# The start of a hybrid attention/state-space block: first three projection units in written order, squares of x moved behind the splits, column table loaded first from another queue

## The chip, the cores and the metric

One core of a Trainium2 chip runs the whole kernel in one launch. The metric is the device time of one execution in microseconds (us), the median of several. Five engines work side by side, each through its own list of instructions in order: TensorE (PE, matrix products, with PEld for the loading of the stationary operand), VectorE (DVE), ScalarE (ACT), GpSimd (POOL) and SyncE (SP, which here only starts DMA transfers). They meet at semaphores.

## The reference

One layer, 512 positions, width 2048, all in float32:

```
u = rmsnorm(x, attn_norm_w)                 # x: 512 x 2048
z, xbc, dt, q, kc, vc, ks, vs, kw, vw, gate = split(u @ w_in)
y_ssd = ssd_mixer(z, conv4+silu(xbc), softplus(dt))    # chunked state-space scan, 16 heads
y_att = nsa_mixer(q, kc, vc, ks, vs, kw, vw, gate)     # compressed + selected + window attention
h = x + concat(y_ssd, y_att) @ w_out
v = rmsnorm(h, ffn_norm_w)
h = h + (silu(v @ w_gate) * (v @ w_up)) @ w_down       # hidden width 5632
return rmsnorm(h, final_norm_w)

rmsnorm(x, w) = x * rsqrt(mean(x*x over the width) + 1e-6) * w
```

The change touches only the first line and the first products `u @ w_in`.

## The kernel before, in words

**Numbers as two halves.** A float32 product is made of three products of a shorter type: each operand is split into a high part (ScalarE writes it, helper `a_hi`, L124) and a low part, the operand less its high part (VectorE, helper `lo`, L127). Then hi·hi, hi·lo and lo·hi are added up in PSUM (L234, L235, L236).

**The input projection.** x is held transposed, as 16 blocks `xt[:, k]` of 128 features by 512 positions. The norm's weight is a column table (`colc`, loaded from `cols`): `u_hi[k]` is the high part of x times its column (ScalarE, L124 `u<-xt,colc`), `u_lo[k]` the rest (VectorE, one scalar_tensor_tensor, L1818, which is L1843 in the changed kernel). The other factor of the norm, one number for each position, is applied after the product: `rms_stats` turns the sum of squares of x into the row `rrow` (flag "r1": four tiny products L282, then L283, a power on GpSimd L285, four transposes L289, a copy L290), and every result is multiplied by `rrow` as it leaves PSUM.

**Units.** The columns of `w_in` are taken in units of 128 (`run_unit`). A unit runs 16 steps k of three matmuls 128x128x512, 48 in all, into one PSUM bank: units 0 and 1 into the two banks `ps_t`, 2 and 3 into `ps_s`, from 4 on alternately into the two banks `ps_g`. The weights come in sub-blocks of 4 k (`wraw`, 256 KB, four buffers); `issue_split` splits one into `whi` and `wlo` (four buffers each) up to three sub-blocks ahead of the matmuls. From the seventh unit on, a unit first needs the unit two before it to have left its bank. Unit 0 holds dt and the gates, unit 1 is B, unit 2 C, units 3 to 6 the x columns of the state-space part's first group, and so on.

**Leaving PSUM.** A unit's `evac` is a generator that `Sched` advances by one step ("tick") after each k of the units that follow. All of them wait for "r1". For unit 0 it ends in a chain of small operations on `dtmp`; for units 1 to 12 it is a convolution of four taps (`conv`: `xpad<-ps,rrow`, then `cv`), a silu, splits and transposes. When these are there, the state-space core and the compression run as further generators between the matmuls.

**What sets the order.** The program is written down in one pass, and a scheduler of the framework then orders the instructions of each engine by its own simulation, except inside `manual_schedule`, where an engine keeps the written order. Before the change, the whole start is left to the scheduler, and PE's order is fixed from unit 25 on (`n_att`); the feed-forward part is fixed for all engines.

**The start before.** SP starts the transfers one after the other: the first weights, x block 0, the column table, x block 1, then pairs of x blocks with weights between. The squares of x are summed into `acc1` (ScalarE squares, GpSimd adds: even k) and `accb` (VectorE squares and adds: odd k), and the scheduler mixes these with the splits.

Of the kernel before, what the change touches and what calls it, by code (L numbers as in the profile page):

```python
# [8 lines left out]
F32 = mybir.dt.float32  # L9
F32R = mybir.dt.float32r  # L10
AF = mybir.ActivationFunctionType
ALU = mybir.AluOpType
AX = mybir.AxisListType

S, D, FF = 512, 2048, 5632
KD = D // 128
# [19 lines left out]
C_AN, C_FN, C_LN, C_SN, C_CW, C_CB, C_PE, C_W2 = 0, 16, 32, 48, 56, 104, 116, 148  # L36
# [29 lines left out]
U_Z = list(range(17, 25))  # L66
# [48 lines left out]
def body(ctx, tc, xT, w_in, w_out, w_gate, w_up, w_down, w1k, w1v, cols, rows, kst, out):  # L115
    nc = tc.nc
    act, dve, pool, pe = nc.scalar, nc.vector, nc.gpsimd, nc.tensor
    sch = Sched()

    def f(ap):  # L120
        return ap.bitcast(F32)

    def a_hi(dst, src, scale=1.0):
        act.activation(dst, src, AF.Copy, scale=scale)  # L124

    def lo(eng, dst, src, hi):
        eng.tensor_tensor(dst, src, f(hi), ALU.subtract)  # L127
# [4 lines left out]
    def mul(eng, o, a, b):  # L132
        eng.tensor_tensor(o, a, b, ALU.mult)  # L133

    def add(eng, o, a, b):
        eng.tensor_tensor(o, a, b, ALU.add)  # L136
# [8 lines left out]
    def ps_g():  # L145
        return ps("g", 2)

    def ps_s():
        return ps("s", 2)

    def ps_t():
        return ps("t", 2)
# [4 lines left out]
    def ps_m():  # L157
        return ps("m", 1)
# [11 lines left out]
    def open_pool(name, stack=None, **kw):  # L170
        es = ExitStack()
        pools[name] = (es, es.enter_context(tc.tile_pool(name=name, bufs=1, reuse_waits="tile", **kw)))
        return pools[name][1]

    def close_pool(name):
        pools.pop(name)[0].close()
# [18 lines left out]
    def issue_dma(upto):  # L195
        while st["dma"] <= min(upto, len(subs) - 1):
            i = st["dma"]
            src, n = subs[i]
            raw[i] = wp.tile([128, KSUB, 128], F32, tag="raw", name="wraw", bufs=4)
            nc.sync.dma_start(raw[i][:, :n, :], src)  # L200
            st["dma"] += 1

    def issue_split(upto):
        while st["split"] <= min(upto, len(subs) - 1):
            i = st["split"]
            issue_dma(i)
            n = subs[i][1]
            h = wp.tile([128, KSUB, 128], F32R, tag="whi", name="whi", bufs=4)
            l = wp.tile([128, KSUB, 128], F32R, tag="wlo", name="wlo", bufs=4)
            a_hi(h[:, :n, :], raw[i][:, :n, :])  # L210
            lo(dve, l[:, :n, :], raw[i][:, :n, :], h[:, :n, :])
            hi_t[i], lo_t[i] = h, l
            del raw[i]
            st["split"] += 1
            issue_dma(i + 3)

    def run_unit(u):
        if u.pre:
            u.pre()
        if u.need:  # L220
            sch.run_until(*u.need)
        n_u = st["unit"] = st.get("unit", 0) + 1
        if n_u > 6:
            sch.run_until(("evac", n_u - 2))
        p = ps_t() if n_u <= 2 else ps_s() if n_u <= 4 else ps_g()
        p = p[:, 0:u.cols[1] - u.cols[0]]
        for i, k0, n in u.sub:
            issue_split(i)
            for j in range(n):
                if j == 0:  # L230
                    issue_split(i + LEAD)
                k = k0 + j
                ah, al = [t[:, u.cols[0]:u.cols[1]] for t in u.rhs(k)]
                pe.matmul(p, hi_t[i][:, j, :], ah, start=(k == 0), stop=False)  # L234
                pe.matmul(p, hi_t[i][:, j, :], al, start=False, stop=False)  # L235
                pe.matmul(p, lo_t[i][:, j, :], ah, start=False, stop=(k == u.nk - 1))  # L236
                sch.tick()
            del hi_t[i], lo_t[i]

        def evac():  # L240
            yield from u.evac(p)
            sch.flags.add(("evac", n_u))
        sch.add(evac())


    colc = cst.tile([128, C_W2 + 4], F32, name="colc")
# [3 lines left out]
    rrow = cst.tile([128, 512], F32, name="rrow")  # L250
# [13 lines left out]
    def kcs(a, n):  # L264
        return kc[:, a - K_TRI:a - K_TRI + n]
# [6 lines left out]
    def col(c, n=1):  # L272
        return colc[:, c:c + n]
# [4 lines left out]
    def rms_stats(acc, n, dst, flag, gap=4):  # L278
        nb = acc.shape[1] // 128
        p = ps_m()  # L280
        for i in range(nb):
            pe.matmul(p[:, i:i + 1], acc[:, i * 128:(i + 1) * 128], ones[:, 0:1], start=True, stop=True)  # L282
        dve.tensor_scalar(rst[:, 0:nb], p[:, 0:nb], 1.0 / n, EPS, op0=ALU.mult, op1=ALU.add)  # L283
        r = rst[:, 4:4 + nb]
        pool.tensor_tensor(r, rst[:, 0:nb], nhalf[:, 0:nb], ALU.pow)  # L285
        yield gap
        p = ps_m()
        for i in range(nb):
            pe.transpose(p[:, i * 128:(i + 1) * 128], r[:, i:i + 1].to_broadcast([128, 128]), ident)  # L289
        act.activation(dst, p[:, 0:128 * nb], AF.Copy)  # L290
        sch.flags.add(flag)
# [9 lines left out]
    u_hi, u_lo = U[:, 0], U[:, 1]  # L301
# [244 lines left out]
    acc2 = cst.tile([128, 512], F32, name="acc2")  # L546
# [418 lines left out]
    def win(u):  # L965
        return w_in[u]
# [30 lines left out]
    order = [U_DTG]  # L997
# [6 lines left out]
    units = [Unit(win(u), KD, u_rhs, ev[u], pre=pre_att if u == U_VS[0] else (lambda: pre_ms()) if u == order[-1] else None) for u in order]  # L1004


    def pre_ms():
        P2["ms"] = [(U[:, 0, k], U[:, 1, k]) for k in range(8)]
        sch.run_until(("gp", 7))
        sch.add(ms_in())  # L1010
# [787 lines left out]

    xs = open_pool("xs")
    xt = xs.tile([128, KD, 512], F32, name="xt")  # L1800
    issue_dma(0)
    nc.sync.dma_start(xt[:, 0, :], xT[0])
    nc.sync.dma_start(colc[:, 0:C_PE], cols[:, 0:C_PE])
    nc.sync.dma_start(xt[:, 1, :], xT[1])
    for k in range(2, KD, 2):
        nc.sync.dma_start(xt[:, k:k + 2, :], xT[k:k + 2].rearrange("k p t -> p k t"))
        if k % 4 == 2:
# [1 line left out]
    nc.gpsimd.dma_start(rowc, rows.to_broadcast([128, 48]))  # L1809
    dve.memset(ones, 1.0)  # L1810
    act.activation(nhalf, ones[:, 0:4], AF.Copy, scale=-0.5)
    for k in range(KD):
        if k % 4 == 0:
            issue_split(k // 4)
        t = xt[:, k, :]
        w = col(C_AN + k)
        a_hi(u_hi[:, k, :], t, scale=w)
        dve.scalar_tensor_tensor(u_lo[:, k, :], t, w, f(u_hi[:, k, :]), op0=ALU.mult, op1=ALU.subtract)  # L1818
    acc1 = acc2
    accb = xs.tile([128, 512], F32, name="accb")  # L1820
    for k in range(KD):
        t = xt[:, k, :]
        if k < 2:
            act.activation((acc1, accb)[k], t, AF.Square)
        else:
            sq = xs.tile([128, 512], F32, tag=f"sq{k % 2}", name="sq", bufs=2)
            if k % 2:
                mul(dve, sq, t, t)
                add(dve, accb, accb, sq)
            else:  # L1830
                act.activation(sq, t, AF.Square)
                add(pool, acc1, acc1, sq)
    add(dve, acc1, acc1, accb)
    nc.sync.dma_start(ident, kst[:, 0:K_TRI])
    nc.sync.dma_start(tri, kst[:, K_TRI:K_AM])
    close_pool("xs")
    open_pool("kcp")
    open_pool("ssd")
# [1 line left out]
    sch.add(ssd_core())  # L1840
    sch.add(compress())
    sch.add(attention())
    first = units[0].evac  # L1843

    def ev_first(p):
        yield from rms_stats(acc1, D, rrow, "r1")
        yield from first(p)
    units[0].evac = ev_first
    n_att = order.index(U_Z[4])
    for n, u in enumerate(units[:n_att]):  # L1850
        if n == 4:
            nc.sync.dma_start(kcs(K_AM, NK - K_AM), kst[:, K_AM:NK])
            nc.sync.dma_start(colc[:, C_PE:C_W2], cols[:, C_PE:C_W2])
        run_unit(u)
    with tc.manual_schedule(engines={mybir.EngineType.PE}):
        sch.flags.add("order")
        for u in units[n_att:]:
# [90 lines left out]
```

## Time and profile before

| what | value |
|---|---|
| median of 3 runs | 2232.8 us (2230.76 to 2238.33) |
| the profiled execution | 2233.11 us, of which its span (first to last instruction) is 2231.3 us |
| PE busy | 2158.5 us, 97% of the span |
| DVE / ACT / POOL busy | 1793.7 / 1195.4 / 438.9 us |
| mean granted TensorE clock | 0.991 |
| moved by DMA | 427.14 MB, mean 191 GB/s |

Times are counted from the first instruction of the program. A row of the time line gives start, duration, engine, line, operation, and in brackets the idle time of that engine just before it and what ended it. A row of the table of stretches gives for each engine the busy time and the number of instructions, then the granted clock (PEclk), the mean busy share of the 16 DMA engines and the rate. Starts on PE are exact; ends are modelled, so two neighbouring starts say more than a duration.

### The profile page before, as it was taken

The page shows a single profiled execution, that of the slowest core. Times are in us where ns is not written, and L with a number is a line of the kernel's source. Part 1 is how long each engine was busy: PE and PEld are TensorE (multiplying, and loading weights), DVE is VectorE, ACT ScalarE, POOL GpSimd, SP SyncE. Part 2 cuts the span into 40 slices and gives each one's busy share as a digit, 9 for nine tenths or more (in the row PEclk, how much of TensorE's full clock was granted, in tenths as well). Part 3 has the DMA queues.
Part 4 walks back from the last instruction along what each step waited for, and adds up shares of the span by engine and source line. Part 5 has one row for each costly group of instructions (what it writes and reads, how often), then busy time and mean ns, then how long its engine had stood idle before and what let it go on. Part 6 is the DMA issues. An engine that isn't in the chain of part 4 may idle for free. (4 is left out here: it accounts for less than half of the span.)

```text
span 2231.3 us, 35003 instructions
## 1 busy us (share of the span) xinstructions
PE 2158.5 (97%) x12892; PEld 1897.8 (85%) x12892; DVE 1793.7 (80%) x2821; ACT 1195.4 (54%) x1991; POOL 438.9 (20%) x459
## 2 busy tenths in 40 slices
PE   7999999999999999999999999999999889999996
PEld 5888888888788887888888888888888889999996
DVE  7799766878886658888888888888887777888886
ACT  4564446676666657555555555555555333333453
POOL 2011224324431135000000000000000121211222
PEclk8999999999999999999999999999999999999998
DMA  5212342223464366778888787887878859686974
GB/s 178 92 68 80 116 156 84 75 93 109 140 207 118 105 211 210 228 217 253 230 236 236 218 246 222 254 229 223 243 218 264 319 189 309 201 275 185 297 187 135
DMA packets 174780, 427.14 MB, mean 191 GB/s; under 512 B 17248, under 2 KB 24432, under 8 KB 174608
## 3 DMA queue, kind: packets, MB, share of 16 engines
q1 hardware_dynamic: 101600, 251.97, 32.8%
q0 software_dynamic: 29712, 85.90, 18.8%
q10 hardware_dynamic: 43296, 87.04, 10.9%
q8 instruction: 101, 1.65, 0.3%
q14 instruction: 71, 0.58, 0.1%
HBM read 358.78 MB, written 62.39 MB: 189 GB/s over the span
## 5 line engine op out<-in xcount | busy, mean ns | idle before, releaser
L124 ACT ACTIVATE R<-Z 128x1024 fp32r<-128x1024 f32 (+4 forms) x458 | 415.9, 922 | 440.4 <-DVE Z L136 319.8
L127 DVE TENSOR_TENSOR R<-Z,R 128x1024 fp32r<-128x1024 f32 (+4 forms) x367 | 380.8, 1046 | 30.8 <-ACT R L124 19.6
L234 PE MATMUL ps_g<-u,whi 128*128 128x512 f32 x778 | 320.8, 412 | 0.0
L236 PE MATMUL ps_g<-u,wlo 128*128 128x512 f32 x778 | 306.2, 394 | 0.0
L235 PE MATMUL ps_g<-u,whi 128*128 128x512 f32 x778 | 304.9, 392 | 0.0
L1219 PE MATMUL ps_s<-u,R 128*128 128x512 f32 (+1 forms) x1160 | 252.9, 348 | 6.8 <-ACT A L1429 6.2
L1219 PEld LDWEIGHTS ps_s<-u,R 128*128 128x128 f32 x1160 | 187.7, 188 | 38.2 <-ACT A L1429 11.1
L127 DVE TENSOR_TENSOR wlo<-wraw,whi 128x512 fp32r<-128x512 f32 x211 | 162.0, 769 | 56.1 <-ACT whi L124 54.7
L124 ACT ACTIVATE whi<-wraw 128x512 fp32r<-128x512 f32 x211 | 131.4, 624 | 125.5 <-PE ps_g L235 82.2
L236 PEld LDWEIGHTS ps_g<-u,wlo 128*128 128x128 f32 x778 | 146.1, 188 | 31.8
L234 PEld LDWEIGHTS ps_g<-u,whi 128*128 128x128 f32 x778 | 146.7, 189 | 23.5
L235 PEld LDWEIGHTS ps_g<-u,whi 128*128 128x128 f32 x778 | 147.0, 189 | 21.1
L1219 PE MATMUL ps_t<-u,R 128*128 128x512 f32 (+1 forms) x600 | 131.4, 347 | 0.0
L1219 PE MATMUL ps_g<-u,R 128*128 128x512 f32 x584 | 131.3, 349 | 0.0
L1219 PE MATMUL ps_s<-T,R 128*128 128x512 f32 (+1 forms) x560 | 125.7, 349 | 1.0 <-DVE R L127 1.0
L1219 PE MATMUL ps_g<-T,R 128*128 128x512 f32 (+1 forms) x584 | 126.0, 346 | 0.7 <-DVE R L127 0.7
L1219 PE MATMUL ps_s<-V,R 128*128 128x512 f32 (+1 forms) x568 | 123.2, 347 | 0.0
L124 ACT ACTIVATE R<-A 128x1024 fp32r<-128x1024 f32 (+3 forms) x76 | 70.9, 933 | 85.9 <-DVE A L136 62.6
L127 DVE TENSOR_TENSOR E<-Z,R 128x1024 fp32r<-128x1024 f32 (+1 forms) x91 | 110.9, 1218 | 4.4 <-ACT R L124 4.1
L872 ACT ACTIVATE e<-e,em 128x128 f32<-128x128 f32 (+3 forms) x128 | 71.6, 559 | 76.1 <-DVE em L870 75.5
L136 DVE TENSOR_TENSOR A<-ps_g,A 128x512 f32<-128x512 f32 (+1 forms) x110 | 71.0, 652 | 50.7 <-PE ps_g L1219 38.6
L136 DVE TENSOR_TENSOR Z<-Z 128x1024 f32<-128x1024 f32 (+5 forms) x96 | 105.1, 1094 | 8.1 <-POOL E L136 5.2
(490 smaller groups left out, 5638.1 us busy)
## 6 DMA issues: line engine op xcount, KB each, us to landing
Z<-in_w_up SPq DMA_DIRECT2D x94, 512.0 KB, 5.0
Z<-in_w_gate SPq DMA_DIRECT2D x94, 512.0 KB, 6.5
wraw<-in_w_in SPq DMA_DIRECT2D x164, 256.0 KB, 2.6
g_d<-A ACTq DMA_DIRECT2D x22, 1792.0 KB, 15.1
Z<-in_w_up POOLq DMA_DIRECT2D x37, 512.0 KB, 7.7
Z<-in_w_gate POOLq DMA_DIRECT2D x37, 512.0 KB, 7.4
Z<-in_w_down SPq DMA_DIRECT2D x59, 320.0 KB, 6.2
Z<-in_w_down SPq DMA_DIRECT2D x41, 384.0 KB, 4.2
```

The lines of the kernel that those rows point to most:

```text
L124: act.activation(dst, src, AF.Copy, scale=scale)
L127: eng.tensor_tensor(dst, src, f(hi), ALU.subtract)
L136: eng.tensor_tensor(o, a, b, ALU.add)
L234: pe.matmul(p, hi_t[i][:, j, :], ah, start=(k == 0), stop=False)
L235: pe.matmul(p, hi_t[i][:, j, :], al, start=False, stop=False)
L236: pe.matmul(p, lo_t[i][:, j, :], ah, start=False, stop=(k == u.nk - 1))
L872: act.activation(e[:, 0:L], e[:, 0:L], AF.Exp, scale=-1.0, bias=m[:, 0:1], accum_out=m[:, 1:2])
L1219: pe.matmul(o, w, x, start=start, stop=(k == n - 1 and o is q), skip_group_check=not fresh[0])
```

## The change

1. The load of the column table is written first, and on ScalarE's queue instead of SP's; x blocks 0 and 1 then follow each other on SP.
2. The splits of x and of the first weights, and units 0, 1 and 2, are put inside `manual_schedule` for PE, ScalarE and VectorE: these three engines keep the written order there. First come all splits, with no square among them.
3. The squares of x become a generator, `x_squares`. It writes its first square 16 ticks after its start, which is the end of unit 0, and then one every second tick, beside units 1 and 2; all 16 squares are ScalarE's, all 15 additions VectorE's, into `acc2`. `accb` and GpSimd's seven additions are gone.
4. The statistics of the norm (`rms_stats`) wait for the flag "sq" that `x_squares` sets, instead of following unit 0 at once.

```diff
+    nc.scalar.dma_start(colc[:, 0:C_PE], cols[:, 0:C_PE])
     issue_dma(0)
-    nc.sync.dma_start(xt[:, 0, :], xT[0])
-    nc.sync.dma_start(colc[:, 0:C_PE], cols[:, 0:C_PE])
-    nc.sync.dma_start(xt[:, 1, :], xT[1])
+    for k in range(2):
+        nc.sync.dma_start(xt[:, k, :], xT[k])
...
-    for k in range(KD):
-        if k % 4 == 0:
-            issue_split(k // 4)
-        t = xt[:, k, :]
-        w = col(C_AN + k)
-        a_hi(u_hi[:, k, :], t, scale=w)
-        dve.scalar_tensor_tensor(u_lo[:, k, :], t, w, f(u_hi[:, k, :]), op0=ALU.mult, op1=ALU.subtract)
-    acc1 = acc2
-    accb = xs.tile([128, 512], F32, name="accb")
-    for k in range(KD):
-        t = xt[:, k, :]
-        if k < 2:
-            act.activation((acc1, accb)[k], t, AF.Square)
-        else:
-            sq = xs.tile([128, 512], F32, tag=f"sq{k % 2}", name="sq", bufs=2)
-            if k % 2:
-                mul(dve, sq, t, t)
-                add(dve, accb, accb, sq)
-            else:
-                act.activation(sq, t, AF.Square)
-                add(pool, acc1, acc1, sq)
-    add(dve, acc1, acc1, accb)
     nc.sync.dma_start(ident, kst[:, 0:K_TRI])
     nc.sync.dma_start(tri, kst[:, K_TRI:K_AM])
+
+    def x_squares():
+        yield 14
+        for k in range(KD):
+            yield 2
+            if k == 0:
+                act.activation(acc2, xt[:, k, :], AF.Square)
+            else:
+                sq = xs.tile([128, 512], F32, tag="sq", name="sq", bufs=2)
+                act.activation(sq, xt[:, k, :], AF.Square)
+                add(dve, acc2, acc2, sq)
+        sch.flags.add("sq")
...
+    def ev_first(p):
+        yield from sch.wait("sq")
+        yield 2
+        yield from rms_stats(acc2, D, rrow, "r1")
+        yield from first(p)
...
+    with tc.manual_schedule(engines={mybir.EngineType.PE, mybir.EngineType.Activation, mybir.EngineType.DVE}):
+        for k in range(KD):
+            if k % 4 == 0:
+                issue_split(k // 4)
+            t = xt[:, k, :]
+            w = col(C_AN + k)
+            a_hi(u_hi[:, k, :], t, scale=w)
+            dve.scalar_tensor_tensor(u_lo[:, k, :], t, w, f(u_hi[:, k, :]), op0=ALU.mult, op1=ALU.subtract)
+        sch.add(x_squares())
+        for u in units[:3]:
+            run_unit(u)
+        sch.run_until("sq")
     close_pool("xs")
...
     for n, u in enumerate(units[:n_att]):
...
-        run_unit(u)
+        if n >= 3:
+            run_unit(u)
```

**VectorE, from its first split on.** Names: `wlo` is the low half of a weight sub-block, `u` the low half of an x block, `sq`, `accb` and `acc` belong to the squares. Before:

```order
L127 TENSOR_TENSOR wlo<-wraw,whi 128x512
L1818 SCALAR_TENSOR_TENSOR u<-xt,colc,u 128x512 x2
L133 TENSOR_TENSOR sq<-xt 128x512
L136 TENSOR_TENSOR accb<-accb,sq 128x512
L1818 SCALAR_TENSOR_TENSOR u<-xt,colc,u 128x512 x2
L133 TENSOR_TENSOR sq<-xt 128x512
L127 TENSOR_TENSOR wlo<-wraw,whi 128x512
```

and now, where four such groups stand ahead of the first addition:

```order
L1843 SCALAR_TENSOR_TENSOR u<-xt,colc,u 128x512 x4
L127 TENSOR_TENSOR wlo<-wraw,whi 128x512
L1843 SCALAR_TENSOR_TENSOR u<-xt,colc,u 128x512 x4
L127 TENSOR_TENSOR wlo<-wraw,whi 128x512 x4
L136 TENSOR_TENSOR acc_96<-acc_96,sq 128x512 x2
L127 TENSOR_TENSOR wlo<-wraw,whi 128x512
```

The squares and additions that stood among the `u` rows have moved behind the last of them, two additions to each later weight split.

**ScalarE, from its first instruction on**, as a difference (- before, + now):

```order
+L1801 DMA colc<-in_cols 128x116
 L1811 ACT_TABLE_LOAD
 L1811 ACTIVATE colc<-ones 128x4
 L124 ACTIVATE whi<-wraw 128x512
-L1824 ACTIVATE acc_96<-xt 128x512
-L124 ACTIVATE u<-xt,colc 128x512 x2
-L1824 ACTIVATE accb<-xt 128x512
-L124 ACTIVATE u<-xt,colc 128x512 x2
-L1831 ACTIVATE sq<-xt 128x512
```

The load of the column table now stands at the head of ScalarE's list, and no square is left between the first `u` rows.

**PE, around the statistics of the norm (L282).** Before, in unit 1 (bank `ps_t`), after 90 large matmuls:

```order
L235 MATMUL ps_t<-u,whi 128x512
L236 MATMUL ps_t<-u,wlo 128x512
L282 MATMUL ps_m<-ones,acc_96 128x1 x4
L234 MATMUL ps_t<-u,whi 128x512
L235 MATMUL ps_t<-u,whi 128x512
```

and now in unit 3 (bank `ps_s`), after 160:

```order
L236 MATMUL ps_s<-u,wlo 128x512
L234 MATMUL ps_s<-u,whi 128x512
L282 MATMUL ps_m<-ones,acc_96 128x1 x4
L235 MATMUL ps_s<-u,whi 128x512
L236 MATMUL ps_s<-u,wlo 128x512
```

The statistics, and with them everything that waits for "r1", stand 70 large matmuls later in PE's list.

More of the change, by code (lines that the diff above doesn't have):

```diff
@@ L1811, in body @@
     act.activation(nhalf, ones[:, 0:4], AF.Copy, scale=-0.5)
-    for k in range(KD):
-        if k % 4 == 0:
-            issue_split(k // 4)
-        t = xt[:, k, :]
-        w = col(C_AN + k)
-        a_hi(u_hi[:, k, :], t, scale=w)
-        dve.scalar_tensor_tensor(u_lo[:, k, :], t, w, f(u_hi[:, k, :]), op0=ALU.mult, op1=ALU.subtract)
-    acc1 = acc2
-    accb = xs.tile([128, 512], F32, name="accb")
-    for k in range(KD):
-        t = xt[:, k, :]
-        if k < 2:
-            act.activation((acc1, accb)[k], t, AF.Square)
-        else:
-            sq = xs.tile([128, 512], F32, tag=f"sq{k % 2}", name="sq", bufs=2)
-            if k % 2:
-                mul(dve, sq, t, t)
-                add(dve, accb, accb, sq)
-            else:
-                act.activation(sq, t, AF.Square)
-                add(pool, acc1, acc1, sq)
-    add(dve, acc1, acc1, accb)
     nc.sync.dma_start(ident, kst[:, 0:K_TRI])
     nc.sync.dma_start(tri, kst[:, K_TRI:K_AM])
+    def x_squares():
[9 more added lines that the diff above has]
+        sch.flags.add("sq")
+    first = units[0].evac
+    def ev_first(p):
[3 more added lines that the diff above has]
+        yield from first(p)
+    units[0].evac = ev_first
+    n_att = order.index(U_Z[4])
+    with tc.manual_schedule(engines={mybir.EngineType.PE, mybir.EngineType.Activation, mybir.EngineType.DVE}):
[10 more added lines that the diff above has]
+        sch.run_until("sq")
     close_pool("xs")
@@ L1842, in body @@
     sch.add(attention())
[L1843 to L1849, printed above, removed]
     for n, u in enumerate(units[:n_att]):
```

## The prediction

> **What bounds the kernel now.** I read the page first, for the engine that is always busy, and then a table of stretches, for where it is not.
>
> ```profile
> PE 2158.5 (97%) x12892; PEld 1897.8 (85%) x12892; DVE 1793.7 (80%) x2821; ACT 1195.4 (54%) x1991; POOL 438.9 (20%) x459
> PEclk8999999999999999999999999999999999999998
> ```
> ```profile
> 0.00:32.00 32.00, 17.00 (x37) 11.15 (x38) 25.09 (x29) 20.27 (x34) 10.32 (x12) 0.74 0.66 226
> 32.00:100.00 68.00, 68.00 (x315) 56.23 (x313) 46.52 (x103) 29.55 (x46) 1.04 (x1) 0.99 0.29 100
> 100.00:200.00 100.00, 100.00 (x517) 83.86 (x516) 87.60 (x169) 52.28 (x82) 12.91 (x9) 1.00 0.22 77
> 200.00:331.00 131.00, 131.00 (x688) 111.15 (x685) 104.06 (x211) 62.25 (x117) 33.52 (x40) 1.00 0.37 124
> 331.00:345.00 14.00, 12.34 (x77) 10.17 (x77) 7.48 (x15) 8.12 (x19) 7.90 (x9) 1.00 0.25 81
> ```
>
> PE bounds the kernel, and the change touches the one stretch where it does not: in the first 32 us PE runs 37 large matmuls, at a granted clock of 0.74, and then has no pause until 331 us. The list of PE's waits up to 50 us says on whom:
>
> ```profile
> PE ps_t L234 <- ACT u L124: 7.7, 1, 7.7
> PE ps_t L235 <- DVE u L1818: 7.3, 4, 3.0
> ```
>
> So PE first waits 7.7 us for the first `u_hi`, then for `u_lo` from VectorE. The time line shows why VectorE is late (POOL's adds are the first and the last of seven; the last DVE row but one is the last `u_lo`):
>
> ```profile
> 10.94 1.42 POOL L136 TENSOR_TENSOR acc<-acc,sq 128x512 f32<-128x512 f32 x1 [8.89 <-ACT sq L1831]
> ...
> 23.03 1.30 POOL L136 TENSOR_TENSOR acc<-acc,sq 128x512 f32<-128x512 f32 x1 [0.39 <-ACT sq L1831]
> ```
> ```profile
> 9.07 0.68 DVE L133 TENSOR_TENSOR sq<-xt 128x512 f32<-128x512 f32 x1
> ...
> 13.43 1.76 DVE L127 TENSOR_TENSOR wlo<-wraw,whi 128x512 fp32r<-128x512 f32 x1
> ...
> 26.01 2.06 DVE L1818 SCALAR_TENSOR_TENSOR u<-xt,colc,u 128x512 fp32r<-128x512 f32 x3
> ...
> 33.66 0.74 DVE L1818 SCALAR_TENSOR_TENSOR u<-xt,colc,u 128x512 fp32r<-128x512 f32 x1
> 34.32 1.88 DVE L127 TENSOR_TENSOR wlo<-wraw,whi 128x512 fp32r<-128x512 f32 x3
> ```
>
> A VectorE operation of this size costs 0.68 to 0.74 (in a row 0.69 for a `u_lo`, 2.06/3, and 0.63 for a weight split, 1.88/3), but 1.76 when it meets one of POOL's adds; seven adds make seven such operations. The last `u_lo` comes at 33.66 + 0.74 = 34.4 us, because squares and POOL's adds stand in its way.
>
> **Part 1: unit 0.** Three floors for the last `u_lo`, k = 15.
>
> ```profile
> 0.00:10.00 10.00, 2.32 (x5) 1.53 (x6) 3.09 (x6) 5.71 (x9) 0.95 (x5) 1.00 0.78 237
> 8.83:12.24 3.41, 3.41 (x8) 2.29 (x8) 3.31 (x5) 3.30 (x7) 1.30 (x1) 1.00 1.05 392
> ```
> ```profile
> 9.68 0.37 SPq L1806 DMA_DIRECT2D xt<-in_xT  x1
> ```
> ```profile
> xt<-in_xT SPq DMA_DIRECT2D x1, 512.0 KB, 9.5
> ```
> ```profile
> 4.47 0.63 ACT L1824 ACTIVATE acc<-xt 128x512 f32<-128x512 f32 x1
> 6.91 1.46 ACT L124 ACTIVATE u<-xt,colc 128x512 fp32r<-128x512 f32 x2 [1.81 <-DMA colc<-in_cols]
> 9.00 1.33 ACT L124 ACTIVATE u<-xt,colc 128x512 fp32r<-128x512 f32 x2
> ```
>
> - DMA: the last pair of x blocks is issued at 9.68 and lands 9.5 later, at 19.2. ScalarE then needs 1.33 for two `u_hi`, VectorE 0.74 for the last `u_lo`: 21.2.
> - VectorE: from the 34.4 of today I take the seven long operations' excess, 7 x 1.07 = 7.5, and the eleven squares and additions that stand ahead of the last `u_lo` (9.07 is the first), some 0.62 each as a row of them goes, 6.8. That leaves 20.1.
> - ScalarE: 16 x 0.67 and four weight splits of 0.63 are 13.2 us of work; it starts near 4.6, so 17.8.
>
> DMA is last, if only by 1 us. How much earlier x comes is the unknown of this part. The column table's load leaves SP's list, so each later start there moves up by one issue (0.42); nothing else in it changes place but one weight load that now precedes the 832 KB table. Today block 0 is there by 4.47 and the column table at 6.91: at most these 2.4 us could come off every later landing. At least 0: the bytes are the same. The DMA engines are idle for 22% of the first 10 us, 2.2 us, of which most is before any packet runs, and full from 8.83 on (1.05). So I sit near the low end, at 0.7. By the Trainium skill ("DMA: Bandwidth & Descriptors", section "Issuing engines are not separate DMA queues") transfers started from different engines interleave on the same 16 DMA engines, and only the starting engine's time is saved; by that alone it would be 0 and the forecast 0.7 later, which the full share of 1.05 supports and the idle 2.2 us does not.
>
> ScalarE's DMA issue ahead of its table load costs nothing: it idles until its first weights land at 3.84 anyway. So the last `u_lo` comes at 21.2 - 0.7 = 20.5, and two matmuls of 0.23 later unit 0 ends, at 21.0.
>
> PE must keep up for that. The granted clock by stretches:
>
> ```profile
> 12.24:15.65 3.41, 1.39 (x5) 0.49 (x3) 3.41 (x4) 3.41 (x7) 2.14 (x3) 1.00 1.04 386
> 22.48:25.89 3.41, 2.62 (x7) 1.47 (x5) 3.41 (x4) 1.55 (x3) 1.46 (x2) 0.50 0.00 0
> 29.30:32.72 3.42, 3.42 (x10) 2.65 (x9) 3.42 (x6) 0.63 (x1) 0.00 (x0) 0.50 0.21 77
> 32.72:36.13 3.41, 3.41 (x16) 2.80 (x16) 3.41 (x7) 0.63 (x1) 0.00 (x0) 1.00 0.02 8
> ```
>
> ```profile
> 9.49 0.63 PE L234 MATMUL ps_t<-u,whi 128*128 128x512 f32 x1
> ...
> 9.91 0.63 PE L235 MATMUL ps_t<-u,whi 128*128 128x512 f32 x1
> ```
>
> Behind a stretch that PE filled (29.30 to 32.72, and 8.83 to 12.24 above) the clock is full, behind one filled to 77% (22.48) it stays at half, and behind one filled to 41% (12.24 to 15.65) it falls to half. (Up to 12.24 the trace has no record of the clock, so it prints 1.00; starts 0.42 to 0.43 apart, as at 9.49 and 9.91, are those of the half clock.) At half clock a step k takes 3 x 0.43 = 1.28 us. Fifteen x blocks come between 6.9 and 19.2, one each 0.82 us. So a half-clocked PE falls behind, is never idle, and gets its full clock within two stretches of 3.4 us. Its 15 steps from k = 1 can start at 8.4 (block 1's `u_hi` of today, 6.91 + 1.46). If it warms at 12.2, as it did before, 3 steps are done by then and 12 x 0.68 = 8.2 bring it to 20.4, within the 21.0 that x allows; if it warms at 15, 5.2 steps are done and it ends at 21.7. So the clock costs 0 to 0.7; I take 0.
>
> **Part 2: units 1 and 2.** At full clock a unit takes 69.54 - 58.65 = 10.89 us:
>
> ```profile
> 58.65 0.39 PE L234 MATMUL ps_s<-u,whi 128*128 128x512 f32 x1
> ...
> 69.54 0.39 PE L234 MATMUL ps_g<-u,whi 128*128 128x512 f32 x1
> ```
>
> Beside the 21.8 us of two units ScalarE has eight weight splits and 16 squares, 24 x 0.63 = 15.1, and VectorE eight splits and 15 additions, 23 x 0.63 = 14.5. Both fit, and the splits lead by up to three sub-blocks, 8 us, which hides a pair of squares between two of them. Unit 1's first split stands right behind the last `u` on both engines, so its low half is there at 20.5 + 0.6 = 21.1, and PE wants it for its third matmul at 21.5. ScalarE has taken over seven squares for this (16 instead of 9), VectorE does 15 additions instead of 7 products and 8 additions, and POOL's seven additions are gone; none is on PE's path any more, save the last, for "r1" (part 3). Unit 3 then starts at 21.0 + 21.8 = 42.8, against 58.65 today. But today's PE has by then also run the small matmuls of the statistics and of unit 0's end:
>
> ```profile
> 44.43 0.95 PE L282 MATMUL ps_m<-ones,acc 128*128 128x1 f32 x8
> ...
> 51.00 0.60 PE L289 MATMUL ps_m<-ident,rst 128*128 128x128 f32 x4
> ...
> 57.45 0.46 PE L319 MATMUL ps_m<-ident,dtg 64*128 64x64 f32 x4
> ```
>
> These 2.0 us come later now. PE is ahead by 58.65 - 2.0 - 42.8 = 13.9 us.
>
> **Part 3: what "r1" holds.** L282 stands 16 matmuls into unit 3: 42.8 + 3.6 = 46.4, against 44.43. So everything that waits for "r1" starts 2.0 us later than today, while PE is 13.9 ahead.
>
> ```profile
> 52.26 0.68 DVE L133 TENSOR_TENSOR dtg<-ps_t,rrow 64x512 f32<-64x512 f32 x1 [1.52 <-ACT rrow L290]
> ...
> 80.62 0.69 DVE L133 TENSOR_TENSOR xpad<-ps_g,rrow 128x512 f32<-128x512 f32 x1 [1.58 <-PE ps_g L236]
> ```
> ```profile
> 53.00:260.00 207.00, 207.00 (x1040) 173.25 (x1040) 179.00 (x361) 101.89 (x159) 25.99 (x18) 1.00 0.23 78
> ```
>
> The banks first. Unit 6 needs unit 4's bank read (`xpad<-ps_g`). It starts near 42.8 + 3 x 10.89 + 2.0 = 77.5. VectorE's chain starts at 54.3, and some 25 operations stand between in its new list, at 0.63 some 16 us: 70, and unit 4 itself ends at 66.6. That is early enough by 7 us. Then VectorE as a whole: from 53 to 260 us it works 179 of 207 us. Now the same work has 207 - 13.9 - 2.0 = 191 us, a load of 94%. It fits if most of the 28 us of idle time were waits for units that now come sooner, like the 1.58 at 80.62. PE's large matmuls keep their lead of weight splits, so VectorE's delay first hits the state-space steps, which the scheduler has put later in PE's list. For new waits between 43 and 345 I take 0.8, half of the 1.66 that PE idles at 331 to 345 today; the ends are 0 and 12 (next part). Behind that, the order on all engines is as before.
>
> **The sum**, against the profiled execution's own 2233.1 us (span 2231.3; the median of the three runs is 2232.8): 2233.1 - 13.9 + 0.8 = 2220.0.
>
> **The rivals.**
> ```profile
> 140.00:150.00 10.00, 10.00 (x59) 8.56 (x58) 10.00 (x23) 7.16 (x11) 1.04 (x1) 1.00 0.23 80
> ```
> - *VectorE gives it back.* If 20 of the 28 us of idle stay, the stretch takes 179 + 20 = 199 us instead of 191, and 8 of the 13.9 go: 2228. For it: the load of 94%. Against it: from 140 to 150 us VectorE doesn't rest today, and PE has no pause there.
> - *PE stays at half clock through unit 0*, since x comes in pairs and leaves pauses. Then the 45 matmuls from k = 1 on, which can't start before 8.4 today (6.91 + 1.46), end 45 x 0.43 = 19.3 later, at 27.7 instead of 21.0: 2226.7. Against it: the arithmetic of 1.28 against 0.82 above. By the Trainium skill ("TensorE: Matmul & The Clock Gate", section "What's actually happening") one busy window of some 3.4 us frees the clock; the rows above agree.
> - *POOL is not the cause of the long operations*, the transfers of x are. Then 7.5 us stay in VectorE's floor, 27.6, and unit 0 ends at 28.1 or so: 2227. Against it: at 9.07 a square took 0.68 with the DMA engines full.
> - *Slower.* The scheduler puts the state-space matmuls into PE's fixed list by a simulation; where VectorE reaches their operands (`ml`, `ptl` and their like) later than PE reaches them, PE stands. This erases the gain once VectorE idles as long as today, 28 us, from its later start: 2.0 us slower, 2235; from 35 us of idle on it is over 0.3%. That needs units that come 13.9 us sooner to make it wait no less.
>
> **How the numbers follow.** 0.3% of the time is 6.7 us; less can't be told from no change. My forecast, with the unknown landing (0 to 2.4) and 0 to 4 of new waits, is 2217 to 2223 and has 0.70. The half clock has 0.07, POOL 0.04, VectorE's giving back 0.12, of which a quarter still under 2226.1; slower 0.03; a greater gain than 16 us 0.04. Faster by over 0.3%: 0.70 + 0.04 + 0.03 + half of the half clock's, 0.81; within it 0.15; slower by over it 0.04. The range leaves out the gain over 16 and the far half of the rivals: 2217 to 2227.
>
> **What will show it.** Right: no VectorE operation over 0.8 us before 42; the first `u_hi` near 5 instead of 6.9; the last `u_lo` at 19 to 22; unit 3's first matmul at 41 to 44; L282 near 46; a clock of 1.0 from 15 us on; PE without a pause over 1 us between 44 and 331. Wrong: pauses of PE behind VectorE between 60 and 260, or x landing no earlier while ScalarE's queue is held up by its own transfer.

## The result

The changed kernel took 2221.5 us (median of 6 runs, 2218.81 to 2225.28) against 2234.16 (6 runs, 2230.76 to 2238.47) for the kernel before on the same chip: a ratio of 0.9946, 95% interval 0.9932 to 0.9961. It was run again in two more groups, each with the kernel before beside it: 0.9957 [0.9942, 0.9973] and 0.9958 [0.9945, 0.9971]. So it is faster, by 0.4 to 0.55%, some 10 to 13 us. One run of the kernel before in the last of these groups, 3030.71 us at a clock of 0.653, is left out; the median of the other 16 is 2233.47. The profiled execution took 2223.84 us (span 2222.1), 2.3 above its median.

### The profile page after: what moved, and what is told of

Same layout as the page of the kernel before. It is cut to its first block, busy times and chain, and to the rows that moved or that the text cites. A ratio compares the mean times of both kernels' runs of the same rounds, so it can differ in the third digit from the quotient of the medians.

```text
span 2222.1 us, 35009 instructions
## 1 busy us (share of the span) xinstructions
PE 2158.5 (97%) x12892; PEld 1898.4 (85%) x12892; DVE 1786.8 (80%) x2821; ACT 1199.3 (54%) x1998; POOL 429.9 (19%) x452
## 5 line engine op out<-in xcount | busy, mean ns | idle before, releaser
L235 PE MATMUL ps_g<-u,whi 128*128 128x512 f32 x778 | 305.3, 392 | 0.0
L235 PEld LDWEIGHTS ps_g<-u,whi 128*128 128x128 f32 x778 | 147.3, 189 | 21.1
```

## The profile after

The page's row of busy time, and the table of stretches (us, then busy time and count of PE, PE's weight loads, VectorE, ScalarE and POOL, then granted clock, DMA share, GB/s):

```profile
PE 2158.5 (97%) x12892; PEld 1898.4 (85%) x12892; DVE 1786.8 (80%) x2821; ACT 1199.3 (54%) x1998; POOL 429.9 (19%) x452
```
```profile
0.00:32.00 32.00, 25.50 (x92) 19.17 (x93) 21.88 (x34) 23.24 (x38) 0.95 (x5) 1.00 0.81 278
32.00:100.00 68.00, 68.00 (x315) 56.24 (x314) 45.61 (x106) 30.63 (x51) 1.04 (x1) 1.00 0.27 94
100.00:200.00 100.00, 100.00 (x532) 84.72 (x531) 95.31 (x185) 58.84 (x89) 14.41 (x10) 1.00 0.21 72
200.00:331.00 131.00, 128.75 (x676) 108.42 (x675) 95.97 (x201) 60.89 (x121) 36.97 (x46) 0.99 0.37 125
```

PE's total is the same to 0.1 us (2158.5). Only its place changed: in the first 32 us it now runs 92 matmuls instead of 37, while POOL's adds are gone (0.95 us instead of 10.32). In the row from 200 on PE has 2.25 us of pauses and a mean clock of 0.99. These are the pauses that the kernel before has at 331 to 345 us (1.66 there, at a clock of 1.00); they now come earlier. PE's waits up to 60 us have one entry, the start and the second x block; VectorE is no longer in the list:

```profile
PE ps_t L234 <- ACT u L124: 6.5, 2, 5.8
```

The time line of the steps that the prediction named (start, duration, engine, line):

```profile
5.02 0.72 ACT L124 ACTIVATE u<-xt,colc 128x512 fp32r<-128x512 f32 x1
...
17.91 2.69 ACT L124 ACTIVATE u<-xt,colc 128x512 fp32r<-128x512 f32 x4 [0.18 <-DMA xt<-in_xT]
...
18.67 2.76 DVE L1843 SCALAR_TENSOR_TENSOR u<-xt,colc,u 128x512 fp32r<-128x512 f32 x4
```
```profile
43.87 0.39 PE L234 MATMUL ps_s<-u,whi 128*128 128x512 f32 x1
...
47.49 0.95 PE L282 MATMUL ps_m<-ones,acc 128*128 128x1 f32 x8
...
56.12 0.39 PE L234 MATMUL ps_g<-u,whi 128*128 128x512 f32 x1
```
```profile
55.33 0.68 DVE L133 TENSOR_TENSOR dtg<-ps_t,rrow 64x512 f32<-64x512 f32 x1 [1.07 <-ACT rrow L290]
...
68.72 0.68 DVE L133 TENSOR_TENSOR xpad<-ps_g,rrow 128x512 f32<-128x512 f32 x1
```

The first `u_hi` comes at 5.02 instead of 6.91, the last `u_lo` at 18.67 + 2.76 = 21.43 instead of 34.40, with four in a row at 0.69 each. Unit 3 starts at 43.87 instead of 58.65. Unit 4, whose `ps_g` bank unit 6 will use, has it read at 68.72; unit 6 starts at 78.50.

To follow the lead further I count the units' 128x512 matmuls (`u` times `whi` or `wlo`). The 145th is unit 3's first. The 1200th is near 346 us, behind the pauses of that region, and in both kernels it has 478 other matmuls of PE ahead of it. Before it started at 356.3, after at 346.0:

```profile
356.31 0.48 PE L236 MATMUL ps_g<-u,wlo 128*128 128x512 f32 x1
```
```profile
346.01 0.48 PE L236 MATMUL ps_g<-u,wlo 128*128 128x512 f32 x1
```

So 10.3 us are gained there. The rest of the program is ordered alike; the two profiled executions drift against each other by 2 to 3 us in it, and end 9.2 apart.

## The experiments

Three groups ran on three chips (x; y; b and z), each with the kernel before beside it on the same chip (2233.57, 2231.55 and 2233.47 us; 35, 23 and 16 runs). The row "the change" is from the result above. The first group has no run of the changed kernel of its own, so its medians are set against those of the other groups, which is good to a few us only. All diffs are against the changed kernel, but for that of b1. Ratios are to the kernel before of the same group. The last three columns are read from each run's own trace (us); z2 has 476 other matmuls ahead of the 1200th, the rest have 478.

| run | median us (runs) | ratio [95%] | last `u_lo` ends | unit 3 starts | 1200th large matmul |
|---|---|---|---|---|---|
| kernel before | | 1 | 34.40 | 58.65 | 356.3 |
| the change | 2221.5 (6) | 0.9946 [0.9932, 0.9961] | 21.43 | 43.87 | 346.0 |
| x1_table_third | 2225.29 (12) | 0.9968 [0.9954, 0.9981] | 21.49 | 43.94 | 344.6 |
| x2_squares_among | 2228.95 (12) | 0.9983 [0.9968, 0.9998] | 29.26 | 52.62 | 353.4 |
| x3_gpsimd_back | 2233.42 (12) | 1.0000 [0.9987, 1.0014] | 32.15 | 55.95 | 356.7 |
| x4_free_order | 2225.47 (12) | 0.9970 [0.9958, 0.9982] | 25.38 | 48.28 | 348.9 |
| y1_changed_again | 2221.87 (6) | 0.9957 [0.9942, 0.9973] | 21.61 | 44.06 | 346.3 |
| y2_table_third_again | 2222.06 (9) | 0.9957 [0.9940, 0.9974] | 21.11 | 43.58 | 344.2 |
| y3_rows_later | 2220.72 (12) | 0.9955 [0.9940, 0.9969] | 21.15 | 43.57 | 344.2 |
| y4_two_units_rows_later | 2219.85 (8) | 0.9955 [0.9938, 0.9971] | 25.05 | 42.81 | 344.9 |
| b1_before_no_gpsimd | 2230.11 (11) | 0.9986 [0.9975, 0.9998] | 27.95 | 52.01 | 354.9 |
| b2_changed_third_time | 2223.57 (6) | 0.9958 [0.9945, 0.9971] | 21.62 | 44.13 | 346.3 |
| z2_two_units_x_first | 2219.98 (6) | 0.9941 [0.9925, 0.9957] | 24.02 | 41.78 | 343.7 |

**The column table's place** (x1, and the same kernel again as y2):

```
-nc.scalar.dma_start(colc[:, 0:C_PE], cols[:, 0:C_PE])
 ... x block 0
+nc.sync.dma_start(colc[:, 0:C_PE], cols[:, 0:C_PE])
 ... x block 1
```

> The changed kernel with one part undone: the column table is loaded third on SP again. Theory A (the DMA engines are full, the table's place moves no later x block): the first u_hi goes back from 5.0 to about 6.9 us, but the last x blocks land at 19.2 as in the changed kernel, the last u_lo comes at 21.3 to 21.6, unit 3 starts at 43.9 +- 0.5, and the time is that of the changed kernel, 2220 to 2223. Rival B (the early start is worth what it brings forward): all of unit 0 is 1 to 2.4 us later, unit 3 starts at 45 to 46.3, 2223 to 2224.

> The kernel with the column table third on SP again, beside its control. Theory A: within 1.5 us of the changed kernel in this group. Rival B: 3 to 4 us slower than it, as the medians of the two groups so far say (2225.3 and 2221.5); where the trace shows why, the full clock comes later than in the changed kernel's, at 16 us or so.

The first matmul was late, as wanted, and nothing else was. PE's waits up to 60 us in x1:

```profile
PE ps_t L234 <- ACT u L124: 7.9, 1, 7.9
PE ps_t L235 <- DVE u L1843: 0.3, 1, 0.3
```

PE waits 7.9 us for its first operand instead of 5.8, but the last x pair lands at 19.29 (19.23 with the change, 19.14 before), and unit 3 starts 0.07 later. x1's time, 2225.29, missed its 2220 to 2223. In y2 the time is that of its control (2222.06 against y1's 2221.87), and unit 3 starts 0.5 earlier than there. So the traces show that the table's place is worth nothing in unit 0, and I take the 2225.29 for scatter between groups; the times alone, with intervals of some 0.3%, could not tell a few us.

**The squares behind the splits, and POOL** (x2, x3). x2 puts the squares back between the splits, on ScalarE with VectorE's additions; x3 in addition gives half of the additions to POOL, as before:

```
 (x2, behind each u_lo)
+if k == 0: act.activation(acc2, t, AF.Square)
+else: sq = xs.tile(...); act.activation(sq, t, AF.Square); add(dve, acc2, acc2, sq)
 (x3, the additions: odd k on VectorE, even k on POOL)
+add(dve, accb, accb, sq)
+add(pool, acc2, acc2, sq)
```

> The changed kernel with the squares put back among the splits, one square (ScalarE) and one addition (VectorE) behind each k, still without GpSimd; the statistics stay behind unit 2. Theory A (VectorE's load ahead of the last u_lo sets unit 0's end): 16 x 0.69 + 3 x 0.62 + 15 x 0.61 = 22 us from 5.8, so the last u_lo at 28 to 29.5 instead of 21.4, unit 3 starts at 51 to 52.5 instead of 43.9, time 2228 to 2230. Rival B (the squares' place costs nothing, the whole gain was GpSimd's collisions): last u_lo near 22, 2222 to 2223.

> As the kernel with the squares among the splits, but the additions of even k are GpSimd's again (seven), and those of odd k VectorE's. Theory A (a two-operand VectorE operation waits for GpSimd's addition, 1.07 us each): VectorE has 17 us of own work ahead of the last u_lo and 7.5 us of such waits, so it comes at 30 to 31.5, later than with all additions on VectorE (28 to 29.5), although VectorE does seven fewer; seven VectorE operations of 1.7 to 1.8 us; time 2229 to 2232. Rival B (the long operations of before came from x's transfers): no operation over 0.8, last u_lo at 23 to 24, 2223 to 2225.

x3's time line of VectorE, around POOL's additions:

```profile
15.90 1.77 DVE L136 TENSOR_TENSOR accb<-accb,sq 128x512 f32<-128x512 f32 x1
17.59 1.40 DVE L1832 SCALAR_TENSOR_TENSOR u<-xt,colc,u 128x512 fp32r<-128x512 f32 x2
...
21.22 2.41 DVE L1832 SCALAR_TENSOR_TENSOR u<-xt,colc,u 128x512 fp32r<-128x512 f32 x2
...
26.59 0.68 DVE L136 TENSOR_TENSOR accb<-accb,sq 128x512 f32<-128x512 f32 x1
```

The same addition takes 1.77 or 0.68, and a pair of `u_lo` 2.41 or 1.40: a VectorE operation that meets one of POOL's loses about 1.05. There are seven of 1.3 us or more in x3, six of them 1.75 to 1.78, and none in x2 or in the change. (x3's last `u_lo`, 32.15, and its time, 2233.42, lie a little above what was expected, and x2's unit 3 by 0.1.) The waits of PE for `u_lo` up to 60 us, x2's and then x3's:

```profile
PE ps_t L235 <- DVE u L1831: 5.2, 12, 0.9
```
```profile
PE ps_t L235 <- DVE u L1832: 5.7, 5, 2.8
```

x3's clock falls back to half, as before's did: its mean up to 32 us is 0.84, x2's 1.00.

```profile
0.00:32.00 32.00, 19.39 (x45) 11.31 (x46) 23.98 (x27) 23.80 (x41) 11.48 (x12) 0.84 0.67 231
```

At the 1200th matmul, x3 to x2 is 3.3 us (POOL's part) and x2 to the change 7.4 (squares behind the splits). By the medians it is 4.5 between x3 and x2, in one group, and 5.4 to 7.5 between x2 and the change, across groups. With both undone the whole gain is gone (1.0000).

**The written order** (x4): the first three units are left to the scheduler.

```
-with tc.manual_schedule(engines={PE, Activation, DVE}):
+if True:
```

> The changed kernel without the written order: the framework's scheduler orders the first three units again, with all else as changed (no GpSimd, squares written behind the splits). It puts nine additions ahead of the last u_lo. Theory A (the written order is worth what stands ahead of the last u_lo): 9 x 0.61 = 5.5 us more on VectorE, less the 1 to 2 us it waits for x today, so the last u_lo at 24.5 to 26, unit 3's 48 matmuls start 3 to 5 us later, 2224 to 2226. Rival B (GpSimd's collisions were all that mattered, the scheduler fills PE as well): 2221 to 2222.5.

```profile
PE ps_t L235 <- DVE u L1843: 2.5, 5, 0.9
```

PE waits 2.5 us for `u_lo`, five times; unit 3 starts 4.4 later, 0.8 of it because L282 stands ahead of it there. At the 1200th 2.9 us of the gain are missing. By the medians it is 1.9 to 4.0, but against other groups; in its own group x4 has the time of x1 (2225.47 and 2225.29), which keeps the written order. So the price of the free order is shown by the traces, not by the times.

**The control** (y1) stands in the table. 

> The changed kernel itself, as the control of this group. Theory A (the time of a kernel scatters by a few us between groups of runs, and the 2225.3 of the kernel with the column table third is such scatter): 2221 to 2225, and no more than 1.5 us from that kernel in this group. Rival B (the early start of PE is worth time that one trace doesn't show): 2220 to 2222.5, and 3 to 4 us faster than it.

**An earlier x** (y3). The broadcast of a small row table occupies the DMA engines at the start; it is moved behind x:

```
-nc.gpsimd.dma_start(rowc, rows.to_broadcast([128, 48]))
 ... load of tri
+nc.sync.dma_start(rowc, rows.to_broadcast([128, 48]))
```

> The changed kernel with the small table of rows (rowc, 24 KB, broadcast) loaded by SP behind x instead of by GpSimd at the start. Theory A (the DMA engines lose some 2 us before 7 us to this load's slow packets: x block 1 lands 2.8 us behind block 0, where a block takes 0.7 later on): block 1 lands at 5.5 to 6.3 instead of 7.7, the last blocks 1.4 to 2.1 earlier than 19.2, the last u_lo at 19.3 to 20 instead of 21.4, unit 3 starts at 42.2 to 43, time 1 to 2 us under the control. Rival B (the first transfers are slow of themselves): all landings within 0.4 of the changed kernel's, time as the control's.

The stretch from 4 to 6 us, with the change (y1) and then with the row table moved:

```profile
4.00:6.00 2.00, 0.40 (x1) 0.29 (x1) 1.11 (x2) 1.35 (x2) 0.00 (x0) 1.00 0.87 83
```
```profile
4.00:6.00 2.00, 0.25 (x1) 0.26 (x1) 0.96 (x2) 1.66 (x3) 0.00 (x0) 1.00 0.93 348
```

The DMA engines count as busy in both, but move 83 GB/s with the table's small packets and 348 without. Block 1 of x lands at 5.55 instead of y1's 7.89. Yet the last lands at 18.95, only 0.5 earlier than y1's 19.41, and y2, with the row table where it was, has 18.92. So this expectation was wrong: the 2.3 us don't carry over to the end of the list. The traces show where they go, not why: the pair behind block 1 lands 1.4 earlier than in y1 (7.88, 9.26), the weights behind that 0.5 (9.46, 9.93). The time is the control's (2220.72, 2221.87).

**Two units at once** (y4, z2). Units 0 and 1 run together over k, so that PE has six matmuls for each x block. Both also have the row table moved as in y3, and the squares beside unit 2. y4 loads the second unit's first weights ahead of x, z2 behind x's first two blocks:

```
 per k: split; 3 matmuls of unit 0; +3 matmuls of unit 1   (weights of both loaded in turn)
 z2: issue_dma(0); x blocks 0, 1; +unit 1's first weights (its k = 0, 1 run behind unit 0's k = 1)
```

> As the one with the rows later, and units 0 and 1 run together: behind each x block's split six matmuls, three for each unit, so that PE has 1.36 us of work for each 0.85 us of x; the squares follow beside unit 2, more densely. Theory A (after the change PE's rest at the start is its wait for x): PE is full from 6.5 on and warms by 10 to 15 us, units 0 and 1 end at 28.5 to 30 instead of 33.0, unit 3 starts at 39.5 to 41 instead of 43.9, and the time is 3 to 4.5 us under the control. Rival B (VectorE, loaded to 94% behind, takes no more): the start is as early, but PE pauses between 60 and 330 us give it back, time within 1 us of the control.

> Units 0 and 1 together and the rows' load later, but x blocks 0 and 1 ahead of the second unit's first weights: the first matmul at 5.8 instead of 7.0, full clock by 12 to 15 us, units 0 and 1 end at 30 to 31 instead of 31.9 (33.0 in the changed kernel), unit 3 starts at 41 to 42 instead of 43.9, the time is 2 to 3 us under the control. Rival (the last x block, which now lands at 21.5 because of the added weights, sets the end): units 0 and 1 end at 31.5 or later, time 1 to 2 us under the control.

y4's first matmul came at 7.03 and its 96th at 31.71 (the control's: 32.95), so unit 3's start missed its 39.5 to 41 by 1.8, and the time, 2.0 under the control's, its 3 to 4.5. The weights had pushed x back: the last pair lands at 21.51. In z2 the first matmul is at 5.77, the 96th at 30.68, as expected, and the only wait of PE up to 60 us is the start:

```profile
PE ps_t L1865 <- ACT u L124: 5.8, 1, 5.8
```

Unit 3 starts 2.35 earlier than in its control (41.78 against 44.13). The time is 3.6 us under the control's by the medians; the intervals (0.9925 to 0.9957, 0.9945 to 0.9971) overlap. It is the lowest ratio here, but that it beats the change is not settled.

**POOL alone, in the kernel before** (b1, against the kernel before), and the control of that group (b2):

```
-add(pool, acc1, acc1, sq)
+add(dve, acc1, acc1, sq)
```

> The kernel before with one part of the change alone: GpSimd's seven additions are VectorE's, the scheduler still orders the start and the column table is still third. Theory A (seven collisions of 1.07 us with GpSimd, and what stands ahead of the last u_lo, set the start): twelve squares and additions remain ahead of it, 7.66 + 16 x 0.67 + 3 x 0.62 + 12 x 0.61 = 27.6, so it comes at 27.5 to 28.5 instead of 34.4, no VectorE operation over 0.8 us, 4 to 7 us under the kernel before. Rival B (the long operations were caused by the transfers of x): long operations stay, 0 to 2 us. Rival C (without the written order nothing is gained, PE being ordered around the late low halves): last u_lo at 28, but unit 3 starts less than 3 us earlier.

> The changed kernel as the control of this group: 2220 to 2224, 10 to 13 us under the kernel before.

The last `u_lo` ends at 27.95, 6.4 earlier, though VectorE has seven additions more; no operation of it is over 1 us there. So POOL was the cause of the long ones. The time is 3.4 us under the kernel before, short of the 4 to 7 expected (and b2, 9.9 under, just short of its 10 to 13). Of the 6.6 us at unit 3, 0.6 are small matmuls that only come later: at the 200th large matmul, where both kernels have 16 others ahead, the lead is 6.0. At the 1200th only 1.4 are left. PE's waits from 60 to 260 us, and the stretch from 53 on, which tell where some of them went:

```profile
PE ps_t L499 <- DVE pf L136: 1.0, 2, 0.7
PE ps_t L499 <- DVE xx L127: 1.0, 1, 1.0
```
```profile
53.00:260.00 207.00, 204.93 (x1033) 170.64 (x1032) 177.54 (x360) 102.36 (x160) 26.09 (x18) 1.00 0.23 77
```

PE stands 2.07 us behind VectorE in the state-space steps, which neither the kernel before nor the change does. From the 1100th matmul to the 1150th, where b1 has a half clock (330.46 to 333.87 us) as the change has one (below), 1.5 are lost. The other 1.0 of the 4.6 I can't place.

## Why the prediction was right, step by step

2220.0 was forecast, 2221.5 measured. The two other groups put the gain at 9.7 and 9.9 us, not 12.7, so 13.1 was 0.4 to 3.4 us too much, and the trace says where.

- **Unit 0 ends with x, not with VectorE.** Right. Both parts are needed: POOL's additions cost 3.3 us at the 1200th matmul, and the squares among the splits 7.4 (x3, x2). The long operations were POOL's (x3, b1), by which that rival falls. PE itself is close behind as a floor, though: in the profiled execution it has no pause over 0.15 from the second x block on, runs 0.8 to 1.5 behind `u_lo` from k = 3 to 11, and starts its last L235 0.23 behind the last `u_lo` (21.66, 21.43). In y1, with the full clock from 12.13, it does wait for the `u_lo` of k = 8 and 12, 0.29 each.
- **How much earlier x lands** was mis-sized: 0.7 by the prediction, 0 measured (19.23 against 19.14).

```profile
9.76 0.37 SPq L1806 DMA_DIRECT2D xt<-in_xT  x1
```
```profile
xt<-in_xT SPq DMA_DIRECT2D x1, 512.0 KB, 9.5
```

  The last pair is issued at 9.76 instead of 9.68 and lands 9.5 later, as before. x1 and y2 move the table back and x lands no later (19.29; 18.92 against y1's 19.41). So one half of the prediction's last sign of being wrong came true; the other did not, as ScalarE had its first `u_hi` at 5.02. The trace agrees here with the section of the Trainium skill that the prediction weighed ("DMA: Bandwidth & Descriptors", "Issuing engines are not separate DMA queues"), and not with me; its sum was 0.7 later. The chain behind the last pair is as worked out: `u_hi` ends 1.37 later (1.33), `u_lo` 0.83 after that (0.74). Unit 1 started at 22.11 instead of 21.0.
- **The clock in unit 0.** Right: full from 14.84 on, near the later of the two cases worked out, which was put at 0.7. It cost next to nothing: unit 1 starts 0.68 behind the last `u_lo`, and in y1, with the full clock from 12.13, 0.69 behind it. The rival of a half clock throughout falls. The rows show it filling up:

```profile
8.01:11.42 3.41, 2.91 (x6) 1.78 (x7) 2.31 (x4) 2.60 (x5) 0.00 (x0) 1.00 1.05 395
11.42:14.84 3.42, 3.42 (x10) 2.65 (x9) 3.42 (x6) 3.23 (x6) 0.00 (x0) 1.00 1.05 389
14.84:18.25 3.41, 3.41 (x17) 2.78 (x16) 3.40 (x6) 3.21 (x6) 0.00 (x0) 1.00 1.05 384
```

  The stretch that PE filled to 85% was followed by one of ten matmuls, still the half clock's pace; that one was filled, and 17 followed. (The 1.00 of the first two rows stands where no clock is on record.)
- **Units 1 and 2 at 10.89 each.** Right: 22.11 to 43.87 is 21.76. With the 2.0 us of small matmuls that come later, PE was ahead by 58.65 - 2.0 - 43.87 = 12.8 instead of 13.9; the 1.1 are unit 0's.
- **What "r1" holds.** Right: L282 at 47.49 (46.4 expected, and 1.1 of it from unit 0), `dtg` at 55.33 (54.3), unit 4's bank read at 68.72 (70).
- **VectorE's tighter load.** The rival that VectorE gives it back did not occur, and the step's own condition held:

```profile
53.00:260.00 207.00, 207.00 (x1052) 173.71 (x1051) 178.14 (x364) 105.55 (x165) 28.75 (x21) 1.00 0.24 82
```

  PE has no pause there. From `dtg` to the first read of z (`zs<-ps_g`) VectorE took 208.23 us before and 191.23 now, as worked out:

```profile
52.26:260.49 208.23, 208.23 (x1047) 174.22 (x1046) 179.74 (x362) 102.50 (x160) 25.99 (x18) 1.00 0.23 78
```
```profile
55.33:246.56 191.23, 191.23 (x974) 160.66 (x973) 171.84 (x356) 97.86 (x154) 25.71 (x17) 1.00 0.23 79
```

  Its load there is 90%, not 94%, as part of its work now falls outside: the weight split that stood at 53.47 comes at 39.07. b1 shows that the rival was real: with another order of the same work, PE does wait for VectorE there, 2.07 us. The slower rival, by the state-space matmuls in PE's list, needed just such pauses, and the change has none from 44 to 316 us.
- **New waits and the like, 0.8** was mis-sized. At the 800th large matmul, with 285 others ahead in both kernels, the lead is 13.2 (228.37 against 241.57), a little over the 12.8 at unit 3; at the 1200th it is 10.3. So 2.9 us are lost, most of it near 320 us. 0.6 are longer pauses around the matmuls of the compression (2.25 instead of 1.66). About 1.5 are a clock that I had not thought of: it falls to half there for one stretch. The other 0.8 I can't place.

```profile
318.63:322.04 3.41, 1.75 (x24) 1.20 (x24) 0.98 (x3) 1.24 (x4) 0.53 (x1) 1.00 0.11 43
322.04:325.45 3.41, 3.41 (x22) 2.94 (x19) 2.61 (x9) 2.56 (x8) 2.03 (x4) 0.50 0.07 12
```

  The kernel before went through its pauses, some 11 us later, without that. The runs without the half clock there lose 1.4 between the same two matmuls (x1, y2 and y3), which gives the 1.5. None of these runs set the clock by itself, so its price for the whole time is read from traces only.

In all: 13.9 - 0.8 = 13.1 was forecast, and by the traces it is 12.8 at unit 3 and 10.3 at 346 us. That the first measurement's median lies only 1.5 us from the forecast owes something to scatter: medians of the changed kernel in three groups are 2221.5, 2221.87 and 2223.57.

## What to carry to other kernels

Where the bounding engine waits only at the start, look for what stands ahead of its operands on the other engines, and put there nothing but those operands; work that nobody wants yet fits behind them, if its consumer's due time (here a bank's reading) allows. Two engines that share a job can slow each other: seven additions handed to POOL cost VectorE more than doing them itself would have. And a lead won early must be followed to the end: in b1 4.6 of 6.0 us were gone 300 us later.

## What the runs showed of the hardware

The clock fell to half after a stretch in which PE was busy for 1.75 of 3.41 us (51%), with no pause over 0.98 us. In the kernel before a stretch at 57% was not followed by half clock; 41% (12.24 to 15.65) was:

```profile
329.67:333.08 3.41, 1.96 (x16) 1.50 (x14) 0.87 (x2) 1.75 (x5) 0.52 (x1) 1.00 0.36 124
```

x1 has the same pauses as the change at the same time, but its clock's stretches lie otherwise, and they divide the pauses between two; the clock stays full:

```profile
316.80:320.21 3.41, 2.59 (x14) 1.75 (x14) 1.60 (x3) 1.22 (x3) 0.52 (x1) 1.00 0.51 166
320.21:323.62 3.41, 2.23 (x33) 1.98 (x33) 2.32 (x4) 1.89 (x6) 0.22 (x1) 1.00 0.00 0
323.62:327.04 3.42, 3.42 (x17) 2.81 (x16) 2.31 (x7) 2.05 (x7) 1.91 (x5) 1.00 0.11 19
```

So how the pauses fall into such stretches seems to decide whether they cost some 1.5 us more, and that differs from run to run. But the busy share gives no sharp bound. Over all the traces of this case, stretches of full clock with a share between 47% and 59% went both ways: x1 kept the clock behind one at 47%, and b1 lost it behind one at 59%.

```profile
900.48:903.89 3.41, 1.59 (x9) 1.04 (x7) 3.41 (x4) 2.92 (x5) 0.00 (x0) 1.00 0.27 100
903.89:907.31 3.42, 3.06 (x16) 2.37 (x16) 3.39 (x4) 3.36 (x6) 0.86 (x1) 1.00 0.64 165
```
```profile
562.56:565.98 3.42, 2.00 (x11) 1.65 (x12) 3.09 (x9) 3.04 (x8) 3.28 (x4) 1.00 0.76 249
565.98:569.39 3.41, 3.41 (x10) 2.61 (x10) 2.14 (x8) 2.58 (x7) 1.22 (x2) 0.50 0.46 150
```

PE's ends are modelled, which may account for some of this; what else sets the fall was not tried by itself.

Also unexpected: an x block that lands 2.3 us earlier brought the last one at most 0.5 forward (y3).
